# A two-layer trunk on one core: the first phase's units in another order, dt first in its last quarter

## The chip, the cores and the metric

The kernel runs on one core of one Trainium2 chip. The metric is the device time of one execution in microseconds. The kernel before takes 1793.42 us, the median of 3 runs (1793.3 to 1794.07).

## What is computed

Two layers over 256 tokens of width 2048, one after the other, and a final RMSNorm:

```python
for i in range(DEPTH):                       # 2
    mod = cond @ ada_w[i] + ada_b[i]         # cond = silu(c)
    shift, scale, gate = jnp.split(mod[:, None, :], 3, axis=-1)
    h = rmsnorm(x, norm_w[i]) * (1.0 + scale) + shift
    out = ssd_mixer(h, ...) if i == 0 else mlstm_mixer(h, ...)
    x = x + gate * out
return rmsnorm(x, final_norm_w)
```

The SSD mixer projects h to a gate z (4096), to x (4096), B and C (1024 each) and to dt (64 heads). x, B and C pass a causal convolution of 4 taps and a SiLU. dt passes a softplus; its running sum over a chunk of 128 tokens gives the decay between two tokens. A head's output is (C·B times decay) times x·dt, eight groups of eight heads. Then come the gate silu(z), a norm by group and the output projection. The mLSTM mixer projects to qk, v, o, z and to 16 gate columns, whose running sums and maxima steer the attention of each head. All weights and activations are float32.

## The kernel before

**Work and engines.** A matmul in float32 is done as three: weight and activation are split into a high and a low part, and hi·hi, hi·lo and lo·hi are summed in PSUM. `split` makes `hi` on ACT and `lo = raw - hi` on DVE, for each 128x1024 piece of weights (a weight half, 0.5 MB); `mm` then issues 24 matmuls for it (lines 298 to 300 with 256 columns of tokens, kind "fm", or 309 to 311 with 512 columns, kind "tm"). SP issues all weight loads in one queue, into six `raw` buffers; `hi` and `lo` have four each.

**Modulation.** `cond @ ada_w` is not done by matmuls. A piece of `ada_w` is loaded, and DVE adds it, times one column of cond, to an accumulator (`aacc`, line 82). After the 16 pieces of a column group `total` transposes the accumulator on TensorE (line 238) and sums each of the eight 128x128 blocks with an ACT instruction that accumulates. Its items stand between the weight items, at places that tables (`ADA_AT`, the numbers in `POST`) and the loop of layer 1 fix.

**Phase one.** Layer 0 goes through the contraction in four quarters (`START`). In each quarter nine units (`PRE`: x of groups 0 to 2, z of groups 0 to 2, and the three B·C units, of which unit j serves the two groups 2j and 2j+1) get their share of weights. The first two (`RES`) stay in PSUM banks (`pj`); the other seven leave their partial sums after every quarter, added by DVE to SBUF tiles (`park`), through banks called `ms`. dt's unit, two weight halves and one bank, is put in the last quarter ahead of the unit number `DTPOS`.

**Background.** What follows a unit (`dt_done`, `bc_done`, `xs_done`, `z_fin`, `gen_ssd`) is a generator; after each weight half all live generators take a step (`run_bg`), so their instructions fall between those of the projections. `hold` keeps note of generators that occupy a PSUM bank. The instructions' order on each engine comes from a scheduler that works on this stream. An engine runs its queue strictly in order.

**dt.** `dt_done` computes the bias, `softplus` (13 DVE operations, one exp on ACT), the scan along tokens and the rest of dtrow, sends the running sums to DRAM (`acd`, POOL queue), then transposes them (lines 564 to 566). `gen_rows` loads them back, spread over the partitions (`acb`), and `gen_decay` makes the decay tiles E on ACT.

**Groups.** `bc_done` does the convolution and then the products B·C (line 585), masked to `cbm`. From unit 1 on it waits until the SSD of group 2j-2 is over. `gen_ssd` waits for dt, B·C and x, makes X, E·cbm, the head outputs, the product with silu(z), the squares by token (`token_sq`, line 342), the group's norm (`vs`, POOL's power `rs`, `dg` on DVE, a transpose at line 335), and y.

**Layer change and after.** The last output pass of layer 0 adds gate·out to x (`xT`, DVE) and squares it; `make_h` reduces, takes the root and spreads it, and `h_chunk` makes the activations of layer 1 (`hT`). Layer 1's first phase has four quarters of eight units (`K1`). Its gates unit goes in the last quarter ahead of the first weight item; `gates_done` makes the gate rows on DVE and transposes them (lines 861, 862) three steps later. At the end `OutStat.write` scales four 128x1024 pieces and stores them from SP's queue (line 389).

Of the kernel before, what the change touches and what calls it, by code (L numbers as in the profile page):

```python
# [11 lines left out]
ALU = mybir.AluOpType  # L12

P = 128
# [14 lines left out]
NV = _o  # L29

ADA_AT = [[0, 2, 3, 3, 5, 5, 5, 7], [0, 0, 4, 5, 5, 5, 8, 8], [0, 0, 0, 1, 2, 3, 7, 8]]
DTPOS = 7
START = [4, 4, 4, 4]
K1 = [("o", 0), ("z", 0), ("qk", 0), ("v", 0), ("qk", 1), ("v", 1), ("o", 1), ("z", 1)]
RES1, DEF1, GPOS = 2, 16, 0
PRE = [('x', 0), ('z', 1), ('z', 2), ('x', 2), ('bc', 0), ('bc', 1), ('bc', 2), ('x', 1), ('z', 0)]
RES = 2
RAWB, HIB, E6B = 6, 4, 2
HP_SPLIT = (False, None)
# [11 lines left out]
def trunk_kernel(ctx, tc, xt, vecs, ada, wdt, wss, wso, wgt, wml, wmo, fnw, result):  # L51
    nc = tc.nc
# [70 lines left out]
    items = []  # L123
# [70 lines left out]
    def hold(b, banks):  # L194
        if banks[0].space == PS:
            holding.append(b)
        return b

    slots = {"s4a": 2, "s4b": 2, "s4c": 2}
# [12 lines left out]
    def ada_work(it):  # L212
        layer, key, q, w = it["layer"], it["key"], it["q"], it["w"]
        per = 1024 // w
        if q == 0:
            finish(sums)
            acc_tiles[layer, key] = sp.tile([P, 1024], F32, tag="adaacc", name=nm("aacc"), bufs=1)
        acc = acc_tiles[layer, key][:, 0:w]
        for k in range(2 * per * q, 2 * per * (q + 1)):
            raw = it["raw"][(k // per) % 2][:, (k % per) * w:(k % per + 1) * w]  # L220
            if k == 0:
                vts(acc, raw, cond[:, 0:1], None, ALU.mult)
            else:
                stt(acc, raw, cond[:, k:k + 1], acc, ALU.mult, ALU.add)
        if q != it["nq"] - 1:
            return
        if key < 4:
            spans = [(4 * key, 4), (16 + 4 * key, 4)]
        else:
            spans = [(32 + 8 * (key - 4), 4), (36 + 8 * (key - 4), 4)]  # L230
        def total():
            yield
            sm = sp.tile([P, 8], F32, tag="asum", name=nm("asum"))
            ps = [misc() for _ in spans]
            c = 0
            for t, (o, n) in zip(ps, spans):
                for b in range(n):
                    nc.tensor.transpose(t[:, b * P:(b + 1) * P], acc[:, (c + b) * P:(c + b + 1) * P], ident)
                c += n
            c = 0  # L240
            for t, (o, n) in zip(ps, spans):
                for b in range(n):
                    sl = slice(b * P, (b + 1) * P)
                    act(t[:, sl], t[:, sl], AF.Copy, accum_out=sm[:, c + b:c + b + 1])
                m = mod[layer][:, o:o + n]
                vtt(m, sm[:, c:c + n], vec(f"ab{layer}", o, n), ALU.add)
                c += n
                known.update((layer, o + b) for b in range(n))
                if 16 <= o < 32:
                    stt(amul[layer][:, o - 16:o - 16 + n], m, 1.0, vec(f"nw{layer}", o - 16, n), ALU.add, ALU.mult)  # L250
            yield
        sums.append(spawn(total()))
# [108 lines left out]
    class OutStat(RowStat):  # L361
# [18 lines left out]
        def write(self):  # L380
            r = self.column()
            for i in range(2):
                for tb in range(2):
                    o = self.o[tb][:, 1024 * i:1024 * (i + 1)]
                    if tb:
                        act(o, o, AF.Copy, scale=r[:, 1:2])
                    else:
                        vts(o, o, r[:, 0:1], None, ALU.mult)
                    nc.sync.dma_start(result[tb * P:(tb + 1) * P, 1024 * i:1024 * (i + 1)], o)

    rbt = {}

# [182 lines left out]
    def bc_done(j):  # L575
        def f(banks):
            def g():
                yield from gate_ok(lambda: j == 0 or held[0, 2 * j - 2].over)
                yield from take("s4c")
                bc = sp.tile([P, 4, T], F32, tag="s4c", name=nm("bc"))  # L580
                yield from gen_conv(banks, "scw", "scb", [32 + 2 * j, 33 + 2 * j, 40 + 2 * j, 41 + 2 * j], bc)
# [10 lines left out]
            held["bc", j] = hold(spawn(g()), banks)  # L592
        return f

    taken = set()

    def xs_done(g):
        def f(banks):
# [64 lines left out]
    def gen_ssd(g):  # L663
# [16 lines left out]
        for j in range(2):  # L680
            yield from gate_ok(lambda: (g, j) in E_t)
            E = E_t[g, j]
            vtt(E, E, cbm[g].unsqueeze(1).broadcast_to([P, 4, 384]), ALU.mult)
            yield from lag(2)
            ps = misc()
            for h in range(4):
# [102 lines left out]
    for tok in POST:  # L789
# [9 lines left out]
        for q, cnt in tok[2:]:  # L799
            mine, exq[q] = exq[q][:cnt], exq[q][cnt:]  # L800
            tail = []
            if tok[0] == "op" and q == 0:
                tail = items[n + 7:]
                del items[n + 7:]
            new = items[n:]
            out, e = [], 0
            for i, it in enumerate(new):
                out.append(it)
                while e < len(mine) and (e + 1) * len(new) <= (i + 1) * len(mine):
                    out.append(mine[e])  # L810
                    e += 1
            items[n:] = out + mine[e:] + tail
# [23 lines left out]
    def gates_done(banks):  # L836
        def g():
# [17 lines left out]
            nc.vector.tensor_tensor_scan(G, ip, ip, 0.0, ALU.max, ALU.max)  # L855
            nc.gpsimd.dma_start(Gd, G[0:8, :])
            vtt(lf, bc, G, ALU.add)
            yield from lag(3)
            p1, p2 = misc(), misc()
            for c in range(2):  # L860
                nc.tensor.transpose(p1[:, c * P:(c + 1) * P], lf[:, c * P:(c + 1) * P], ident)
# [133 lines left out]
    for q in range(4):  # L995
# [4 lines left out]
        for j, w in enumerate(new):  # L1000
            if q == 3 and j == GPOS:
                add_unit(Unit("fm", 1, 8, 1, h_act, gates_done), [wgt])
            items.append(w)
            n = -(-len(late) // max(1, len(new) - j + (2 - q) * len(new))) if q < 3 else 0
            items.extend(late[:n])
            late = late[n:]
    assert not late
# [148 lines left out]
```

## Time and profile before

| what | value |
|---|---|
| median of 3 runs | 1793.42 us |
| profiled execution | 1796.28 us, span 1794.2 us |
| mean granted TensorE clock | 0.973 |
| PE busy | 1689.0 us (94%), 13285 matmuls |
| DVE, ACT, POOL busy | 73%, 52%, 2% |
| read from HBM | 400.89 MB, 225 GB/s over the span |
| DMA queue of the loads | 64.1% of 16 engines' span |

The page shows PE near its full share and the other engines well below it. The idle time of DVE and ACT is thus no cost by itself; what counts is the idle time of PE, and who ended it. The granted clock is that of TensorE: 1 is 2.4 GHz, 0.5 is 1.2 GHz. "L82" in a row is a helper's line (`stt`), as are 78 (`act`), 86 (`vtt`) and 90 (`vts`), so rows are told apart by their tiles.

### The profile page before, as it was taken

The numbers are of one execution on the slowest core, as the hardware profiler recorded it, in microseconds if no ns is written. First come the engines' busy times: TensorE is split into PE (matmuls) and PEld (weight loads), VectorE is DVE, ScalarE is ACT, GpSimd is POOL, SyncE is SP. The second block draws the span as 40 slices with busy tenths as digits, with TensorE's granted clock in tenths as the row PEclk, the third lists the DMA queues.
The fourth block names the chain that finished last, engine by engine and source line by source line (L and its number), as shares of the span: only waits on it lengthen the run. The fifth ranks groups of instructions, "written<-read, shape, count | busy, mean of one in ns | idle before, by whom it ended". The sixth has DMA issues, their size and how long they took to land.

```text
span 1794.2 us, 32830 instructions
## 1 busy us (share of the span) xinstructions
PE 1689.0 (94%) x13285; PEld 1632.0 (91%) x13285; DVE 1301.5 (73%) x1635; ACT 928.0 (52%) x1583; POOL 36.2 (2%) x55
## 2 busy tenths in 40 slices
PE   2998999888999999979997999999999999999997
PEld 2998998888999999979897989899999999999996
DVE  6789996888986788677967886767455556564554
ACT  3443557868874674435444554544345444454433
POOL 0000000000000000000000000000000000000000
PEclk6999999989999999989998999999999999999998
DMA  9989855756876667878954666777555555555551
GB/s 358 323 298 302 298 181 181 263 188 207 288 280 212 214 221 252 277 246 302 333 199 138 206 217 228 256 237 238 198 185 173 186 170 186 185 195 175 186 180 69
DMA packets 111048, 405.20 MB, mean 226 GB/s; under 512 B 12440, under 2 KB 12448, under 8 KB 110896
## 3 DMA queue, kind: packets, MB, share of 16 engines
q1 hardware_dynamic: 107856, 392.54, 64.1%
q0 software_dynamic: 3040, 10.56, 1.9%
q8 instruction: 104, 1.70, 0.4%
q14 instruction: 48, 0.39, 0.1%
HBM read 400.89 MB, written 2.17 MB: 225 GB/s over the span
## 4 chain that ended last, share of the span: by engine, by line
PE 72%; issue 10%; DVE 9%; DMA 6%; ACT 2%; POOL 0%; SPq 0%; ACTq 0%; POOLq 0%; DVEq 0%
PE pj L298 17%; PE pj L300 17%; PE pj L299 17%; DMA raw<-in_ada 4%; DVE aacc L82 3%; DVE lo L86 3%; PE ms L298 2%; PE ms L300 2%; PE ms L299 2%; PE pj L309 2%; PE pj L310 2%; PE pj L311 2%; DMA raw<-in_wss 1%; ACT hi L78 1%; PE ms L689 1%
## 5 line engine op out<-in xcount | busy, mean ns | idle before, releaser
L78 ACT ACTIVATE hi<-raw 128x1024 fp32r<-128x1024 f32 x548 | 582.1, 1064 | 677.5 <-PE pj L299 444.0
L86 DVE TENSOR_TENSOR lo<-raw,hi 128x1024 fp32r<-128x1024 f32 x548 | 667.0, 1222 | 333.7 <-ACT hi L78 330.7
L298 PE MATMUL pj<-hT,hi 128*128 128x256 f32 x2144 | 608.2, 284 | 8.0 <-ACT hT L78 6.6
L300 PE MATMUL pj<-hT,lo 128*128 128x256 f32 x2144 | 602.7, 281 | 2.2 <-DVE lo L86 2.2
L299 PE MATMUL pj<-hT,hi 128*128 128x256 f32 x2144 | 601.6, 281 | 0.6 <-DVE hT L82 0.6
L298 PEld LDWEIGHTS pj<-hT,hi 128*128 128x128 f32 x2144 | 406.9, 190 | 11.4 <-ACT hT L78 7.4
L300 PEld LDWEIGHTS pj<-hT,lo 128*128 128x128 f32 x2144 | 406.2, 190 | 3.1 <-DVE lo L86 3.0
L299 PEld LDWEIGHTS pj<-hT,hi 128*128 128x128 f32 x2144 | 406.9, 190 | 1.1 <-DVE hT L82 0.8
L298 PE MATMUL pj<-y,hi 128*128 128x256 f32 x1024 | 292.2, 285 | 0.0
L300 PE MATMUL pj<-y,lo 128*128 128x256 f32 x1024 | 290.3, 283 | 0.0
L299 PE MATMUL pj<-y,hi 128*128 128x256 f32 x1024 | 290.1, 283 | 0.0
L82 DVE SCALAR_TENSOR_TENSOR aacc<-raw,cond,aacc 128x1024 f32<-128x1024 f32 x180 | 230.7, 1281 | 72.8 <-DMA raw<-in_ada 71.6
L298 PE MATMUL ms<-hT,hi 128*128 128x256 f32 x704 | 197.9, 281 | 3.9 <-DVE park L86 2.4
L300 PE MATMUL ms<-hT,lo 128*128 128x256 f32 x704 | 197.1, 280 | 1.7 <-DVE lo L86 1.7
L298 PEld LDWEIGHTS pj<-y,hi 128*128 128x128 f32 x1024 | 196.5, 192 | 1.0 <-issue 0.9
L299 PE MATMUL ms<-hT,hi 128*128 128x256 f32 x704 | 196.8, 280 | 0.0
L299 PEld LDWEIGHTS pj<-y,hi 128*128 128x128 f32 x1024 | 196.7, 192 | 0.0
L300 PEld LDWEIGHTS pj<-y,lo 128*128 128x128 f32 x1024 | 196.7, 192 | 0.0
L298 PEld LDWEIGHTS ms<-hT,hi 128*128 128x128 f32 x704 | 132.4, 188 | 5.9 <-DVE park L86 3.0
L300 PEld LDWEIGHTS ms<-hT,lo 128*128 128x128 f32 x704 | 132.3, 188 | 2.3 <-DVE lo L86 2.3
L299 PEld LDWEIGHTS ms<-hT,hi 128*128 128x128 f32 x704 | 132.4, 188 | 0.4
L309 PE MATMUL pj<-hi,hT 128*128 128x512 f32 x192 | 77.3, 403 | 0.0
(185 smaller groups left out, 1569.7 us busy)
## 6 DMA issues: line engine op xcount, KB each, us to landing
raw<-in_wml SPq DMA_DIRECT2D x256, 512.0 KB, 3.9
raw<-in_ada SPq DMA_DIRECT2D x192, 512.0 KB, 5.4
raw<-in_wss SPq DMA_DIRECT2D x160, 512.0 KB, 4.7
raw<-in_wso SPq DMA_DIRECT2D x64, 512.0 KB, 5.5
raw<-in_wmo SPq DMA_DIRECT2D x64, 512.0 KB, 3.8
acb<-acd POOLq DMA_DIRECT2D x16, 512.0 KB, 5.9
xT<-in_xt SPq DMA_DIRECT2D x4, 512.0 KB, 6.2
out<-o SPq DMA_DIRECT2D x4, 512.0 KB, 4.0
```

The costliest lines, as they stand in the source:

```text
L78: nc.scalar.activation(out, in_, func, **kw)
L82: nc.vector.scalar_tensor_tensor(out, a, s, b, op0, op1)
L86: nc.vector.tensor_tensor(out, a, b, op)
L298: nc.tensor.matmul(o, hi[:, w0:w0 + P], ah, start=first, stop=False, skip_group_check=True)
L299: nc.tensor.matmul(o, hi[:, w0:w0 + P], al, start=False, stop=False, skip_group_check=True)
L300: nc.tensor.matmul(o, lo[:, w0:w0 + P], ah, start=False, stop=last, skip_group_check=True)
L309: nc.tensor.matmul(o, ah[:, s], wh, start=(fresh and kk == 0), stop=False)
L310: nc.tensor.matmul(o, al[:, s], wh, start=False, stop=False)
L311: nc.tensor.matmul(o, ah[:, s], wl, start=False, stop=(kk == u.nk - 1 and (closes or (u.park is not None and ends))))
L689: nc.tensor.matmul(o, X[:, 0, xh, :], E[:, h, 0:T], start=True, stop=False, skip_group_check=True)
```

## The change

`PRE` has another order: x0 and the B·C unit 0 are now the two that stay in PSUM, and the other B·C units and x1 come earlier. `DTPOS` is 0: dt's unit is put ahead of the last quarter's first unit. `hold` moves a generator with a PSUM bank to the front of those that step. `total` sums the shift half of layer 0's groups with one DVE reduction in place of four ACT instructions. B·C unit j waits for the last use of group 2j-2's `cbm`, not for that group's end. The last output pass of layer 0 has modulation only among its first eight weight items of twelve, and layer 1's modulation starts at the fourth unit of its first quarter, not at the first. The gates' transposes come after six steps, not three. The second token half's stores are issued from ACT's queue.

```diff
--- before.py
+++ after.py
@@ -29,11 +29,11 @@
 NV = _o
 
 ADA_AT = [[0, 2, 3, 3, 5, 5, 5, 7], [0, 0, 4, 5, 5, 5, 8, 8], [0, 0, 0, 1, 2, 3, 7, 8]]
-DTPOS = 7
+DTPOS = 0
 START = [4, 4, 4, 4]
 K1 = [("o", 0), ("z", 0), ("qk", 0), ("v", 0), ("qk", 1), ("v", 1), ("o", 1), ("z", 1)]
 RES1, DEF1, GPOS = 2, 16, 0
-PRE = [('x', 0), ('z', 1), ('z', 2), ('x', 2), ('bc', 0), ('bc', 1), ('bc', 2), ('x', 1), ('z', 0)]
+PRE = [('x', 0), ('bc', 0), ('z', 0), ('x', 1), ('bc', 1), ('bc', 2), ('z', 1), ('x', 2), ('z', 2)]
 RES = 2
 RAWB, HIB, E6B = 6, 4, 2
 HP_SPLIT = (False, None)
@@ -194,6 +194,8 @@
     def hold(b, banks):
         if banks[0].space == PS:
             holding.append(b)
+            gens.remove(b)
+            gens.insert(0, b)
         return b
 
     slots = {"s4a": 2, "s4b": 2, "s4c": 2}
@@ -239,7 +241,11 @@
                 c += n
             c = 0
             for t, (o, n) in zip(ps, spans):
-                for b in range(n):
+                both = layer == 0 and key < 4 and c == 0
+                if both:
+                    nc.vector.tensor_reduce(sm[:, 0:n], t.rearrange("p (b t) -> p b t", b=4), axis=mybir.AxisListType.X,
+                                            op=ALU.add)
+                for b in range(0 if both else n):
                     sl = slice(b * P, (b + 1) * P)
                     act(t[:, sl], t[:, sl], AF.Copy, accum_out=sm[:, c + b:c + b + 1])
                 m = mod[layer][:, o:o + n]
@@ -386,7 +392,7 @@
                         act(o, o, AF.Copy, scale=r[:, 1:2])
                     else:
                         vts(o, o, r[:, 0:1], None, ALU.mult)
-                    nc.sync.dma_start(result[tb * P:(tb + 1) * P, 1024 * i:1024 * (i + 1)], o)
+                    (nc.scalar if tb else nc.sync).dma_start(result[tb * P:(tb + 1) * P, 1024 * i:1024 * (i + 1)], o)
 
     rbt = {}
 
@@ -575,7 +581,7 @@
     def bc_done(j):
         def f(banks):
             def g():
-                yield from gate_ok(lambda: j == 0 or held[0, 2 * j - 2].over)
+                yield from gate_ok(lambda: j == 0 or 2 * j - 2 in cb_used)
                 yield from take("s4c")
                 bc = sp.tile([P, 4, T], F32, tag="s4c", name=nm("bc"))
                 yield from gen_conv(banks, "scw", "scb", [32 + 2 * j, 33 + 2 * j, 40 + 2 * j, 41 + 2 * j], bc)
@@ -592,7 +598,7 @@
             held["bc", j] = hold(spawn(g()), banks)
         return f
 
-    taken = set()
+    taken, cb_used = set(), set()
 
     def xs_done(g):
         def f(banks):
@@ -681,6 +687,8 @@
             yield from gate_ok(lambda: (g, j) in E_t)
             E = E_t[g, j]
             vtt(E, E, cbm[g].unsqueeze(1).broadcast_to([P, 4, 384]), ALU.mult)
+            if j:
+                cb_used.add(g)
             yield from lag(2)
             ps = misc()
             for h in range(4):
@@ -802,6 +810,9 @@
             if tok[0] == "op" and q == 0:
                 tail = items[n + 7:]
                 del items[n + 7:]
+            if tok[0] == "op" and ip == npass:
+                tail = items[n + 8:]
+                del items[n + 8:]
             new = items[n:]
             out, e = [], 0
             for i, it in enumerate(new):
@@ -855,7 +866,7 @@
             nc.vector.tensor_tensor_scan(G, ip, ip, 0.0, ALU.max, ALU.max)
             nc.gpsimd.dma_start(Gd, G[0:8, :])
             vtt(lf, bc, G, ALU.add)
-            yield from lag(3)
+            yield from lag(6)
             p1, p2 = misc(), misc()
             for c in range(2):
                 nc.tensor.transpose(p1[:, c * P:(c + 1) * P], lf[:, c * P:(c + 1) * P], ident)
@@ -1001,7 +1012,7 @@
             if q == 3 and j == GPOS:
                 add_unit(Unit("fm", 1, 8, 1, h_act, gates_done), [wgt])
             items.append(w)
-            n = -(-len(late) // max(1, len(new) - j + (2 - q) * len(new))) if q < 3 else 0
+            n = -(-len(late) // max(1, len(new) - j + (2 - q) * len(new))) if q < 3 and (q, j) >= (0, 3) else 0
             items.extend(late[:n])
             late = late[n:]
     assert not late
```

Three places show how the queues change. The first is PE's queue around dt's transposes. In the kernel before (`ms_2944` is a parked unit's bank, `pj` a unit's that stays):

```order
L565 MATMUL ms_2929<-ident,acs 128x128 [waits DVE_49,PE_49]
L298 MATMUL ms_2944<-hT,hi_2793 128x256 [waits PE_49]
L565 MATMUL ms_2929<-ident,acs 128x128 [waits DVE_49]
L299 MATMUL ms_2944<-hT,hi_2793 128x256
L566 MATMUL ms_2929<-ident,dtrow 128x128 [waits DVE_49]
L300 MATMUL ms_2944<-hT,lo_2794 128x256
```

The transposes stand between the matmuls of a unit that has no part in dt. In the changed kernel, where `pj_2256` is dt's own bank and `ms_2493` that of unit z0:

```order
L306 MATMUL pj_2256<-hT,lo_2189 128x256
L570 MATMUL ms_2408<-ident,dtrow 128x128 [waits DVE_49]
L570 MATMUL ms_2408<-ident,dtrow 128x128
L571 MATMUL ms_2409<-ident,acs 128x128 [waits DVE_49] x2
L572 MATMUL ms_2409<-ident,dtrow 128x128 [waits DVE_49]
L304 MATMUL ms_2493<-hT,hi_2363 128x256 [waits Activation_49]
L305 MATMUL ms_2493<-hT,hi_2363 128x256
```

dt's last matmul, the transposes that wait for DVE, and the next unit's matmuls now follow each other directly.

The second place is DVE's queue ahead of the end of the convolution for B·C unit 1 (`bc_3894` before, `bc_3338` in the change; `xs_3857` is the x of group 2, `y` a finished group). Before:

```order
L82 SCALAR_TENSOR_TENSOR bc_3894<-park_649,V,bc_3894 128x255
L82 SCALAR_TENSOR_TENSOR xs_3857<-park_502,V,xs_3857 128x254
L82 SCALAR_TENSOR_TENSOR bc_3894<-park_649,V,bc_3894 128x254
L82 SCALAR_TENSOR_TENSOR xs_3857<-park_502,V,xs_3857 128x253
L82 SCALAR_TENSOR_TENSOR bc_3894<-park_649,V,bc_3894 128x253
L86 TENSOR_TENSOR lo_4046<-raw_3925,hi_4045 128x1024
L82 SCALAR_TENSOR_TENSOR xs_3857<-th_4049,xs_3857 128x512
L82 SCALAR_TENSOR_TENSOR bc_3894<-park_649,V,bc_3894 128x255
L82 SCALAR_TENSOR_TENSOR aacc_3573<-raw_3929,cond,aacc_3573 128x1024
L82 SCALAR_TENSOR_TENSOR bc_3894<-park_649,V,bc_3894 128x254
L82 SCALAR_TENSOR_TENSOR aacc_3573<-raw_3931,cond,aacc_3573 128x1024
L82 SCALAR_TENSOR_TENSOR bc_3894<-park_649,V,bc_3894 128x253
```

In the changed kernel, up to the last row of the convolution:

```order
L86 TENSOR_TENSOR lo_3552<-raw_3321,hi_3551 128x1024
L86 TENSOR_TENSOR xs_2403<-xs_2403,ms_3558 128x1024
L82 SCALAR_TENSOR_TENSOR bc_3338<-park_646,V,bc_3338 128x255
L86 TENSOR_TENSOR lo_3597<-raw_3406,hi_3596 128x1024
L86 TENSOR_TENSOR y_3602<-xs_2403,y_3602 128x4x256
L82 SCALAR_TENSOR_TENSOR bc_3338<-park_646,V,bc_3338 128x254
L82 SCALAR_TENSOR_TENSOR bc_3338<-park_646,V,bc_3338 128x253
L86 TENSOR_TENSOR lo_3639<-raw_3408,hi_3638 128x1024
L82 SCALAR_TENSOR_TENSOR bc_3338<-th_3642,bc_3338 128x512
```

The x convolution and the modulation products that alternated with its steps are gone from this stretch; parts of group 0's end stand there.

The third place is DVE's queue at the layer change, from the last residual add to the `dg` of the new layer's norm. Before:

```order
L82 SCALAR_TENSOR_TENSOR xT<-pj_8971,mod_80,xT 128x256 x2
L86 TENSOR_TENSOR lo_9261<-raw_9082,hi_9260 128x1024
L82 SCALAR_TENSOR_TENSOR aacc_9166<-raw_9164,cond,aacc_9166 128x1024
L354 TENSOR_REDUCE vs_9217<-xss_168 128x2
L82 SCALAR_TENSOR_TENSOR aacc_9166<-raw_9290,cond,aacc_9166 128x1024
L90 TENSOR_SCALAR vs_9217<-vs_9217 128x2
L82 SCALAR_TENSOR_TENSOR aacc_9166<-raw_9292,cond,aacc_9166 128x1024
L90 TENSOR_SCALAR dg_9222<-ones,rs_9220 128x128 x2
```

In the changed kernel:

```order
L82 SCALAR_TENSOR_TENSOR xT<-pj_8991,mod_80,xT 128x256 x2
L82 SCALAR_TENSOR_TENSOR xT<-pj_8992,mod_80,xT 128x256 x2
L86 TENSOR_TENSOR lo_9241<-raw_9019,hi_9240 128x1024
L90 TENSOR_SCALAR aacc_9398<-raw_9270,cond 128x1024
L360 TENSOR_REDUCE vs_9197<-xss_168 128x2
L90 TENSOR_SCALAR vs_9197<-vs_9197 128x2
L90 TENSOR_SCALAR dg_9202<-ones,rs_9200 128x128 x2
```

Of three modulation products one is left, ahead of the reduction, and it is the first of its group.
On PE, further on, the gates' transposes (lines 872 and 873 of the changed kernel) move behind one more "tm" unit of 24 matmuls.

## Rows read from the trace of the kernel before

**Rows 1.** The page: busy time by engine; granted clock in 40 slices.

```profile
PE 1689.0 (94%) x13285; PEld 1632.0 (91%) x13285; DVE 1301.5 (73%) x1635; ACT 928.0 (52%) x1583; POOL 36.2 (2%) x55
...
PEclk6999999989999999989998999999999999999998
```

**Rows 2.** Waits of PE in four stretches (255, 420, 780, 960): total, times, longest us.

```profile
PE pj L300 <- DVE lo L86: 1.6, 2, 0.9
PE pj L298 <- ACT hi L78: 0.8, 1, 0.8
...
PE ms L342 <- DVE xs L86: 6.8, 1, 6.8
...
PE ms L335 <- DVE dg L90: 5.3, 1, 5.3
PE ms L342 <- DVE xT L82: 4.5, 2, 3.9
...
PE ms L861 <- DVE gaterow L86: 10.2, 1, 10.2
```

**Rows 3.** PE's timeline after 353: start, duration, instruction, idle before and its releaser.

```profile
366.40 1.19 PE L585 MATMUL ms<-bc 128*128 128x256 f32 x2 [12.52 <-DVE bc L82]
...
371.23 0.41 PE L300 MATMUL pj<-hT,lo 128*128 128x256 f32 x1
...
371.62 0.28 PE L299 MATMUL pj<-hT,hi 128*128 128x256 f32 x1
```

**Rows 4.** Windows: length, PE, PEld, DVE, ACT, POOL busy, clock, DMA share, GB/s.

```profile
0.00:45.00 45.00, 11.01 (x54) 9.79 (x55) 30.91 (x44) 15.07 (x43) 2.91 (x9) 0.68 0.95 358
...
287.00:294.00 7.00, 5.42 (x31) 5.01 (x31) 3.12 (x3) 7.00 (x17) 0.54 (x1) 0.76 0.38 123
...
315.00:360.00 45.00, 38.88 (x337) 37.72 (x335) 39.82 (x54) 38.75 (x80) 2.36 (x4) 0.98 0.75 257
...
712.00:785.00 73.00, 72.70 (x609) 72.50 (x608) 53.27 (x58) 31.08 (x52) 0.00 (x0) 1.00 0.83 278
...
810.00:870.00 60.00, 56.77 (x429) 53.82 (x429) 47.87 (x50) 31.14 (x52) 0.00 (x0) 1.00 0.91 315
```

**Rows 5.** DVE's timeline at 968, after the unit ahead of the gates' transposes.

```profile
968.00 0.68 DVE L86 TENSOR_TENSOR park<-park,ms 128x512 f32<-128x512 f32 x1
```

**Rows 6.** DVE's timeline at the start of layer 0's activations.

```profile
40.33 1.26 DVE L82 SCALAR_TENSOR_TENSOR htmp<-xT,am,ms 128x256 f32<-128x256 f32 x3
```

**Rows 7.** DVE's timeline of dt's chain, from 257 to 274.

```profile
257.40 0.69 DVE L82 SCALAR_TENSOR_TENSOR bc<-th,bc 128x512 f32<-128x512 f32 x1
258.04 0.48 DVE L90 TENSOR_SCALAR dtrow<-pj,V 128x256 f32<-128x256 f32 x1
...
259.07 1.22 DVE L86 TENSOR_TENSOR lo<-raw,hi 128x1024 fp32r<-128x1024 f32 x1
...
260.53 1.75 DVE L413 RECIPROCAL spw<-spw 128x256 f32<-128x256 f32 x1
...
268.41 0.48 DVE L82 SCALAR_TENSOR_TENSOR xs<-park,V,xs 128x255 f32<-128x255 f32 x1
268.81 0.42 DVE L82 SCALAR_TENSOR_TENSOR spw<-spw 128x256 f32<-128x256 f32 x1
...
273.68 0.73 DVE L555 TENSOR_TENSOR_SCAN acs<-ones,dtrow 128x128 f32<-128x128 f32 x2
```

**Rows 8.** PE's timeline at dt's transposes (no idle time before them).

```profile
273.03 0.41 PE L564 MATMUL ms<-ident,dtrow 128*128 128x128 f32 x2
```

**Rows 9.** DVE's timeline at the layer change.

```profile
786.77 1.28 DVE L82 SCALAR_TENSOR_TENSOR aacc<-raw,cond,aacc 128x1024 f32<-128x1024 f32 x1 [3.54 <-DMA raw<-in_ada]
...
793.01 1.28 DVE L82 SCALAR_TENSOR_TENSOR aacc<-raw,cond,aacc 128x1024 f32<-128x1024 f32 x1
...
797.52 0.48 DVE L90 TENSOR_SCALAR dg<-ones,rs 128x128 f32<-128x128 f32 x2 [0.58 <-POOL rs L326]
```

**Rows 10.** The final stores, line 389: from issue to landing.

```profile
DMA to landing us min/median/max: 2.7/4.0/5.5
```

## The prediction

> **What bounds the kernel now.** I read the page first: TensorE (PE) is busy 1689.0 of 1794.2 us, DVE 73%, ACT 52%, and PE's clock is full in most slices [rows 1]. So time is lost only where PE idles (105 us) or runs at half clock, and the reader should ask of every edit which PE wait it touches. Apart from the head and the final norm it is in few places, which the waits by stretch name: three small waits near 271 to 289, a DVE product before the squares at 426, the layer change near 784 to 799, the gate row at 968 [rows 2], and the longest, 12.52 us before the second group pair's B·C product at 354 [rows 3]. Each long wait is paid twice. PE came back at 366.40 at 1.2 GHz, its matmuls take 0.41 us up to 371.23 and 0.28 from 371.62, when 2.4 GHz is granted again, 5.2 us later [rows 3]. Half of that, 2.6 us, is lost. For waits of 6 to 10 us I take 2 us. The windows give the clock and the traffic of the stretches, and the head: 34 of the first 45 us are idle, while the first modulation is awaited [rows 4].
>
> **Sum base.** Durations are from the profiled execution, 1796.28 us (span 1794.2 and 2.1 around it); it stands 2.9 above the median of 1793.42, and differences carry over. A measurement of this kernel tells about 0.2%, 3.6 us, from no change.
>
> **The start: -0.5.** One 128x512 reduction on DVE replaces four ACT accumulations for the shift half, four times. DVE operations of that width take 0.68 (a park add of a PSUM bank) [rows 5]. But the first `htmp` starts at 40.33 behind a product on its own queue [rows 6], so ACT's shorter queue helps little there. Bounds 0 to -2, value -0.5.
>
> **dt first: +16.8.** Before, dt's chain on DVE runs from 258.04 to 274.41: bias, softplus, a reciprocal of 1.75, scan, with other units' work between [rows 7]. The transposes that wait for it begin at 273.03 and cost PE nothing [rows 8], since over a hundred projection matmuls lie between. In the new order the five transposes stand directly behind dt's own 48 matmuls, ahead of z0's first. So PE has nothing to run while DVE makes dtrow, and the scan too. Between them DVE's queue holds dt's 19 operations, together 8.8 us by their rows, one lo (1.22), nine conv steps (0.48) and three silu products (0.69): 16.4 in all, and since each starts about 0.08 before the one ahead ends (268.41 to the next at 268.81) some 14.2 us. All of it is PE idle, plus 2.6 for the clock: +16.8. Bounds: 8.8 if the foreign rows were done already; 16.4 (the chain as it ran before) plus 2.6, or 19.0. I take the count of the new queue.
>
> **What the early dt buys: -4.1 and -23.9, with +6.0 given back.** Now E and X of the first group come in the pause. Before, they pushed hi and lo conversions out, 1.6 + 0.8 us of waits, and part of 287 to 294 ran at 1.2 GHz (granted 0.76 over 7 us, so 1.7 lost) [rows 2, 4]: -4.1, bound 0. At the second pair's B·C product, DVE interleaved two convolutions and two modulation products. In the new order no xs step stands between, and from the lo that releases PE's last 24 matmuls (712 to 785 has 609 in 72.7 us, 0.12 each [rows 4], so 2.9 us) to the last silu product DVE has four 1.22 rows, three 0.48 and one 0.69, 6.4 us in steps. The wait becomes at most 3.5 if DVE comes straight from that lo; I take 2.8, as part of it lies done by then. So -12.52 - 2.6 = -15.1, and +2.8 back. At 426 the product waited behind the third pair's conv [rows 2]; in the new order that conv lies two hundred PE rows earlier: -6.8 - 2 = -8.8. New small waits: 1 at the third pair's B·C and 2.2 at the first group's `dg` (a `dg` wait can cost 5.3, [rows 2]). So +6.0 of new waits, bounds 0 and 9.
>
> **Layer change: -2.5.** Before, the last residual adds stand behind a modulation product that waits 3.54 us for its load, and products sit between reduction, scale and `dg` (793.01 to 797.52) [rows 9]; PE idles 3.9 + 0.6 + 5.3 us. With the last pass's modulation in its first eight items and layer 1's later, only one product stands ahead of the reduction. The `xT` wait goes nearly whole, two products of 1.2 go out of the chain, but POOL and `dg` remain: -5.5 us, clock left as it is. Against it: each of those eight items now brings 2.1 MB per 5.6 us of matmuls, 374 GB/s. The windows show 358 at a share of 0.95, 278 at 0.83 and 315 at 0.91 [rows 4]. At 358 an item lasts 0.26 longer, 2.1 over eight; at 315 it is 8.5. The share of 0.91 says that 315 was not all, so I take +3, bounds 0 and 8.5. The Trainium skill (DMA: Bandwidth & Descriptors, Where 436 GB/s comes from) gives 425 GB/s for one core whose pair is idle, and about 358 as the limit of HBM per core. By the first the term is 0 and the total 1777, by the second 2; the trace, with 358, agrees with the second.
>
> **Gates: -4.9.** Before, the transposes follow a unit that ends just before 968 and wait 10.2 us [rows 2]. Now one more unit, 24 matmuls of 512 columns, twice the width of the former ones, 24 x 0.24 = 5.7 us, stands ahead of them. DVE's chain grows: one lo more, a park add of 0.68 that waits for that unit, fewer qk steps, some 11.0 instead of 10.2 [rows 5]. The wait becomes 5.3: -4.9, bounds 0 and -7. The half clock stays, as after 426's wait of 6.8.
>
> **Tail: 0.** The four stores land 2.7 to 5.5 us after their issue [rows 10]. ACT must finish both scalings before its two issues, so the last issue hardly comes earlier (-0.5 to +0.3). If a second queue had bandwidth of its own, the last landing could be the shortest, 2.7 instead of 5.5, and the term -2.8. The Trainium skill (DMA: Bandwidth & Descriptors, Issuing engines are not separate DMA queues) says against it that all queues share the same 16 engines and that a second issuer saves issue time alone; no row here shows two store queues.
>
> **Sum:** -0.5 + 16.8 - 4.1 - 15.1 - 8.8 + 6.0 - 2.5 - 4.9 + 0 = -13.1, so 1793.4 - 13.1 = 1780.
>
> **Rivals.**
> 1. *Slower: the pause is not paid back.* dt's stall stands, and DVE, which gains no time in it, is just as late at the second pair's B·C product and at the squares at 426. For it: DVE is busy 39.8 of 45 us from 315 to 360 [rows 4]. Against it: the new queue has no foreign conv before that product. It decides when DVE is more than 12 us behind PE at the second pair. Both waits back, without the 3.8 of new waits there: -13.1 + 23.9 - 3.8 = +7, 1800.
> 2. *The layer and gate edits don't do what they say.* Loads of eight dense items cost 8.5 instead of 3, and the gate wait keeps its 10.2: -13.1 + 5.5 + 4.9 = -2.7, 1790.7. For it: the share is already 0.91 to 0.95 [rows 4].
> 3. *The new small waits don't occur*, as the pause lets ACT and the loads run ahead: -13.1 - 6.0 = -19, 1774. Against it: `dg` and B·C still end on DVE. With dt's stall at its bound of 8.8 + 2.6 it is -24.5, 1769.
>
> **How the numbers follow.** Forecast 0.55, own range 1775 to 1787; rival 1 0.15; rival 2 0.15; rival 3 0.15. The range for 8 in 10 takes rivals 2 and 3 and leaves out most of rival 1 and the best ends: 1767 to 1796. Faster than 1789.8: the forecast, rival 3 and a third of rival 2, so 0.75; within 0.2%: most of rival 2 and some of rival 1, 0.11; slower 0.14.
>
> **What would show it.** In the new trace: one PE wait of 12 to 16 us ended by DVE's dtrow near 230 to 245, with half clock behind it (if under 9, rival 3; if absent, I misread the order). No wait above 4 us at the second pair's B·C product, none above 2 at the squares (if back, rival 1). At the layer change no load wait ahead of the last `xT`, a `dg` wait of 3 to 5, and in the 70 us before it PE waits of 1 to 5 us in all for hi or lo, at over 330 GB/s (if 8, rival 2). At the gates one wait of 4 to 7 us. After some 1060 us all lines should shift by one constant; a difference there would prove the sum wrong.

## The result, and the profile after

The changed kernel takes 1775.13 us, the median of 4 runs (1770.52 to 1779.86), against 1793.74 for the kernel before (4 runs, 1793.3 to 1794.87). The ratio is 0.9895, with a 95% interval of 0.9866 to 0.9925, so 18.6 us faster, 13.5 to 24 by the interval. Measured again beside the experiments it took 1779.64 (6 runs) against 1792.41 (18 runs), ratio 0.9925 (0.9909 to 0.9941), 12.8 us faster. The forecast, 1780 and 13.1 faster, lies inside the second interval and just outside the first; 1780 is also just above the slowest of the first four runs.

The profiled execution is the fastest of the four, 1770.52; that of before, 1796.28, took longer than any of its four. The differences below between these two traces add up to 25.5 us of span, and not to 18.6.

The page of the changed kernel, with the parts that answer to [rows 1]:

```profile
span 1768.7 us, 32784 instructions
...
PE 1679.2 (95%) x13285; PEld 1623.4 (92%) x13285; DVE 1301.9 (74%) x1639; ACT 923.3 (52%) x1551; POOL 35.6 (2%) x55
...
PEclk6999989999999999999999999999999999999998
```

PE's idle time falls from 105 to 89.5 us. Its busy time falls by 9.8 us with the same 13285 matmuls, since fewer of them ran at 1.2 GHz: the mean granted clock is 0.980, against 0.973.

The waits of PE in the stretches of [rows 2], at the places where the program now is (total, times, longest us):

```profile
PE ms L570 <- DVE dtrow L82: 12.9, 1, 12.9
PE ms L571 <- DVE acs L561: 0.2, 1, 0.2
...
PE pj L304 <- DVE xs L82: 2.6, 1, 2.6
PE ms L341 <- ACT hi L78: 0.7, 1, 0.7
PE ms L348 <- DVE xs L86: 0.6, 1, 0.6
...
PE ms L341 <- DVE dg L90: 3.2, 1, 3.2
PE pj L304 <- ACT hT L78: 1.1, 1, 1.1
PE ms L348 <- DVE xT L82: 0.3, 1, 0.3
...
PE ms L872 <- DVE gaterow L86: 5.3, 1, 5.3
```

A 12.9 us wait for dt's row is new. The 12.5 us wait before the B·C product of the second pair is gone, and the waits for the squares' product, the residual adds and the gate row have shrunk from 6.8, 4.5 and 10.2 to 0.6, 0.3 and 5.3.

PE's timeline at dt's transposes (start, duration, instruction, idle before and its releaser):

```profile
239.59 0.69 PE L570 MATMUL ms<-ident,dtrow 128*128 128x128 f32 x2 [12.89 <-DVE dtrow L82]
240.44 0.79 PE L571 MATMUL ms<-ident,acs 128*128 128x128 f32 x2 [0.16 <-DVE acs L561]
241.02 0.42 PE L572 MATMUL ms<-ident,dtrow 128*128 128x128 f32 x1
241.45 0.41 PE L305 MATMUL ms<-hT,hi 128*128 128x256 f32 x1
...
243.36 0.28 PE L305 MATMUL ms<-hT,hi 128*128 128x256 f32 x1
```

Projection matmuls stand behind the transposes. They were ready: in the kernel with later transposes, below, the same matmuls run without a wait until 245. Here they take 0.41 us until 2.4 GHz is granted again at 243.3, 3.7 us after PE resumed: 1.9 us more.

DVE's timeline over that wait:

```profile
226.74 0.48 DVE L90 TENSOR_SCALAR dtrow<-pj,V 128x256 f32<-128x256 f32 x1 [0.20 <-PE pj L306]
227.14 0.47 DVE L82 SCALAR_TENSOR_TENSOR bc<-pj,V,bc 128x254 f32<-128x254 f32 x1
227.53 0.42 DVE L82 SCALAR_TENSOR_TENSOR spw<-dtrow 128x256 f32<-128x256 f32 x1
227.87 1.22 DVE L86 TENSOR_TENSOR lo<-raw,hi 128x1024 fp32r<-128x1024 f32 x1
...
238.51 0.69 DVE L82 SCALAR_TENSOR_TENSOR bc<-th,bc 128x512 f32<-128x512 f32 x1
239.12 0.42 DVE L82 SCALAR_TENSOR_TENSOR dtrow<-dtrow,spw 128x256 f32<-128x256 f32 x1
...
239.96 0.74 DVE L561 TENSOR_TENSOR_SCAN acs<-ones,dtrow 128x128 f32<-128x128 f32 x2
```

dt's operations alternate with steps of two convolutions. From 226.74 to 239.54 DVE has no idle time to speak of; its queue is the wait.

The windows that answer to [rows 4] (columns as there):

```profile
315.00:360.00 45.00, 45.00 (x386) 44.90 (x385) 43.33 (x59) 34.68 (x68) 1.29 (x2) 1.00 0.65 222
...
710.00:750.00 40.00, 40.00 (x338) 39.99 (x337) 32.49 (x33) 16.39 (x30) 0.00 (x0) 1.00 0.94 343
750.00:777.00 27.00, 26.69 (x221) 26.09 (x220) 14.93 (x21) 12.58 (x22) 0.00 (x0) 1.00 0.57 196
```

PE is busy 45.00 of 45 us where it waited for B·C before. In the last pass of layer 0 the loads run at 343 GB/s, share 0.94, and PE is busy for all of 710 to 750.

**Where the time went.** Both traces hold 13285 matmul records on PE. The starts of the n-th in each, worked out from the traces (in the reordered part the n-th are not the same matmul, but the same amount of work stands before it), give the lead that the changed kernel has at that point:

| n | before, us | after, us | lead, us | what lies since the row above |
|---|---|---|---|---|
| 1500 | 229.1 | 225.8 | +3.3 | head and first three quarters |
| 1600 | 240.8 | 252.6 | -11.8 | dt's transposes |
| 2500 | 351.3 | 358.8 | -7.5 | waits at 271 to 289 of before |
| 2600 | 378.5 | 370.3 | +8.2 | B·C product of before at 354 |
| 3500 | 492.0 | 480.3 | +11.7 | squares at 426, the new bank wait at 419 |
| 5500 | 727.7 | 717.7 | +10.0 | a modulation sum at 495 |
| 6200 | 829.2 | 811.2 | +18.0 | layer change |
| 7200 | 966.5 | 950.5 | +15.9 | modulation sums of layer 1 |
| 7400 | 1008.3 | 987.7 | +20.6 | gates |
| 8600 | 1178.6 | 1154.6 | +24.0 | a q·k wait, 2.25 before and 0.85 after |
| end of span | 1794.2 | 1768.7 | +25.5 | rest and tail |

### The profile page after: what moved, and what is told of

Its sections match the earlier page's. It is cut to its first block, busy times and chain, and to the rows that moved or that the text cites. A ratio compares the mean times of both kernels' runs of the same rounds, so it can differ in the third digit from the quotient of the medians.

```text
span 1768.7 us, 32784 instructions
## 1 busy us (share of the span) xinstructions
PE 1679.2 (95%) x13285; PEld 1623.4 (92%) x13285; DVE 1301.9 (74%) x1639; ACT 923.3 (52%) x1551; POOL 35.6 (2%) x55
## 4 chain that ended last, share of the span: by engine, by line
PE 73%; issue 9%; DVE 8%; DMA 7%; ACT 2%; POOL 0%; SPq 0%; POOLq 0%; DVEq 0%; ACTq 0%
PE pj L304 18%; PE pj L305 18%; PE pj L306 18%; DMA raw<-in_ada 4%; DVE aacc L82 3%; DVE lo L86 3%; PE ms L304 2%; PE ms L305 2%; PE ms L306 2%; PE pj L315 2%; PE pj L317 2%; PE pj L316 2%; DMA raw<-in_wml 1%; ACT hi L78 1%; PE ms L697 1%
```

## The experiments

The theory is that PE's waits were moved: dt's transposes cost 15 us, the phase-one reordering gives back more than that, and layer change and gates add to it. The rivals: only the later edits gain; the pause is what lets DVE catch up; the loads limit the layer change. Three kernels undo or shift one thing in the changed kernel, five put one part into the kernel before, three build on what these showed, and one is the changed kernel again.

**The changed kernel again.** No edit.

> The changed kernel once more, to see which waits vary from run to run (its first runs spread over 9 us, those of before over 2). Theory 'phase one on the loads': the spread sits in the stretch from 45 to 230 us, where the loads run at 310 to 340 GB/s; there the time of the same matmul moves by 3 us or more between two profiles and the rest moves little. Theory 'borderline B·C wait': it sits at the second pair's B·C product or the squares after it (0 and 2.6 us in the first profile), where a wait of 3 to 9 us appears. Median 1772 to 1779 in either case.

1779.64 us (1778.65 to 1781.38, 6 runs), 0.6 above the range that I had given. Its trace is 2.3 us behind the first one at n = 1400; the same places lose more, and the bank wait of 2.59 at 419 is now:

```profile
426.53 0.55 PE L304 MATMUL pj<-hT,hi 128*128 128x256 f32 x1 [5.05 <-DVE xs L82]
```

There the lag grows to 5.1 at n = 3200. At 850 to 890 it grows by 1.6, at the q·k product near 1143 by 1.6 (a wait of 2.25 against 0.85), 8.9 at the end. So neither theory holds as it stood. The stretch up to 230 us moved by 2.3 and not by 3, and the rest by more. The wait that grew is not at the B·C product, which stayed at 0, nor at the squares, but at the PSUM bank which the x convolution of a later group still reads. What makes these waits vary was not settled. The kernel before varies too: 1787.24 to 1798.85 over 18 runs here.

**Phase one alone**, in the kernel before:

```diff
-DTPOS = 7
+DTPOS = 0
-PRE = [('x', 0), ('z', 1), ('z', 2), ...
+PRE = [('x', 0), ('bc', 0), ('z', 0), ...
+            gens.remove(b)
+            gens.insert(0, b)
-                yield from gate_ok(lambda: j == 0 or held[0, 2 * j - 2].over)
+                yield from gate_ok(lambda: j == 0 or 2 * j - 2 in cb_used)
```

> The kernel before with the phase-one part alone (order of units, dt first in the last quarter, held generators in front, the earlier release of B·C units). Theory 'moved waits': dt's pause of 13 and its clock cost 15 us, and the waits of before at 271 to 289, 354 and 426 give back 25 or so: 7 to 12 us faster than before, 1782 to 1787. Rival 'only the later edits gain': pause and gain cancel, 1791 to 1796, and the 13 to 15 us of the gain come from the layer change and the gates.

1787.2 us (10 runs), ratio 0.9969 (0.9954 to 0.9984), by the ratio 5.6 us faster. By the median it sits where both ranges nearly meet; the timeline decides for moved waits:

```profile
247.41 0.69 PE L566 MATMUL ms<-ident,dtrow 128*128 128x128 f32 x2 [12.89 <-DVE dtrow L82]
...
429.50 0.36 PE L300 MATMUL pj<-hT,hi 128*128 128x256 f32 x1 [2.62 <-DVE xs L82]
```

The two waits are those of the changed kernel to 0.03 us, the waits at 354 and 426 are gone. What this part gives is less than I expected (7 to 12). The pause is not why: in this trace it costs 15.7 us of lead (n = 1500 to 1600), and 24.4 come back until n = 3200, both as expected. Until n = 3800 4.4 are lost again, in waits for the squares, lo and the modulation (the longest 1.64, at 506), which I had not counted. The trace is that of the slowest of the ten runs, and its head alone is 4.5 behind that of before.

**dt's transposes later**, in the changed kernel:

```diff
             vts(cr, acs[:, 0:P], -1.0, acs[:, P - 1:P], ALU.mult, ALU.add)
-            yield
+            yield from lag(8)
```

> The changed kernel, but dt's transposes eight steps after its scan instead of one, so that some 125 PE rows of projections stand between dt's matmuls and them. Theory 'the transposes alone hold PE': the pause of 12.9 us and its 1.9 us of half clock go, nothing else gets worse by more than 3: 1760 to 1766. Rival 'the pause is what lets DVE catch up': the wait comes back at the first E or at the second pair's B·C product, 5 to 12 us: 1770 to 1776.

1768.9 us (4 runs), 10.7 us less than the changed kernel in the same comparison. PE's timeline:

```profile
245.55 0.38 PE L570 MATMUL ms<-ident,dtrow 128*128 128x128 f32 x2
...
246.69 0.55 PE L571 MATMUL ms<-ident,acs 128*128 128x128 f32 x2 [0.40 <-DVE acs L561]
247.09 0.33 PE L572 MATMUL ms<-ident,dtrow 128*128 128x128 f32 x1
250.43 0.55 PE L304 MATMUL ms<-hT,hi 128*128 128x256 f32 x1 [3.01 <-DVE dtT L90]
...
261.08 0.38 PE L304 MATMUL ms<-hT,hi 128*128 128x256 f32 x1 [1.25 <-DVE cbm L82]
...
269.36 0.36 PE L304 MATMUL ms<-hT,hi 128*128 128x256 f32 x1 [1.53 <-ACT hi L78]
...
417.21 0.35 PE L304 MATMUL pj<-hT,hi 128*128 128x256 f32 x1 [2.24 <-DVE xs L82]
```

The 12.89 us wait is gone. 3.01 stay: a unit waits for the bank that the transposes filled and DVE has not read. Two more follow, 1.25 for the mask of B·C and 1.53 for hi, where the changed kernel waits 0.9 at most. Against the second trace of the changed kernel this one is 15.0 us ahead at n = 1600, and 8.2 of them are gone again at n = 1800. So the pause was a loss on balance, but the rival has a part: without the pause some work behind it comes late. The waits further on do not grow. At the bank of the x convolution (2.24 here, 5.05 in that trace, 2.59 in the first) 5.6 more are gained, at a place that varies between executions. The time lies between the two expected ranges, 3 us above the first; the wait for the transposes' bank, and the two behind it, were not in it. Against the first four runs of the changed kernel it is 6.2 us less, and not 10.7.

**dt's unit back in its old place**, all else changed:

```diff
-DTPOS = 0
+DTPOS = 7
```

> The changed kernel with dt's unit put back ahead of the eighth unit of the last quarter, all else as changed. Theory 'the order of the units frees DVE at the B·C product, the early dt costs': the pause goes, no wait over 4 us at the second pair's B·C product, small hi and lo waits of 2 to 5 us near 290 come back: 1762 to 1770. Rival 'the early dt is what moves E and X out of the way of the convolutions': a wait of 8 us or more at the B·C product or the squares: 1775 to 1785.

1782.26 us (5 runs), 2.6 slower than the changed kernel beside it. No 12.9 us wait, but these:

```profile
294.51 0.58 PE L304 MATMUL pj<-hT,hi 128*128 128x256 f32 x1 [3.37 <-ACT hi L78]
...
412.83 1.22 PE L591 MATMUL ms<-bc 128*128 128x256 f32 x2 [2.10 <-DVE bc L82]
...
424.10 1.94 PE L348 MATMUL ms<-ident,xs 128*128 128x128 f32 x8 [4.41 <-DVE xs L86]
...
430.96 0.55 PE L304 MATMUL pj<-hT,hi 128*128 128x256 f32 x1 [4.93 <-DVE xs L82]
```

14.8 us of waits, each with its half clock, against 12.9 + 2.6 + 0.6 with dt early. The product at 412 is that of the third pair. The rival has the time, neither has the mechanism: the 12.5 us wait at the second pair did not come back, so with the earlier release its absence does not need the early dt; but without the early dt PE waits some 12 us more at 291 to 431, nearly what the transposes cost with it. This trace, of the slowest of the five runs, is 15.7 us ahead of the second trace of the changed kernel at n = 1800 and 3.5 behind it at n = 3200. In the medians, dt early takes 2.6 us off this kernel, and 13.4 with the transposes later as well.

**The old release of the B·C units**, all else changed:

```diff
-                yield from gate_ok(lambda: j == 0 or 2 * j - 2 in cb_used)
+                yield from gate_ok(lambda: j == 0 or (0, 2 * j - 2) in held and held[0, 2 * j - 2].over)
```

> The changed kernel, but B·C unit j waits again for the whole end of group 2j-2 (all else as changed). Its second convolution then alternates with the x convolution of group 2 again on DVE. Theory 'the earlier release is what keeps the two convolutions apart': PE waits 5 to 11 us at the second pair's B·C product near 365 and up to 3 for the clock, so 1783 to 1790. Rival 'the order of the units and the early dt do it': no wait over 4 us there, 1775 to 1780.

1784.84 us (4 runs), 5.2 more than the changed kernel's 1779.64, which was measured in another comparison; the kernel before took 1792.59 here and 1792.41 there. The time is in the first theory's range, the wait is elsewhere:

```profile
431.16 0.55 PE L304 MATMUL pj<-hT,hi 128*128 128x256 f32 x1 [9.98 <-DVE xs L82]
```

DVE's timeline ahead of that:

```profile
421.59 0.48 DVE L82 SCALAR_TENSOR_TENSOR bc<-park,V,bc 128x255 f32<-128x255 f32 x1
...
424.26 1.25 DVE L82 SCALAR_TENSOR_TENSOR xs<-pj,V,xs 128x255 f32<-128x255 f32 x3
```

PE waits 9.98 us, not at a B·C product but for the PSUM bank which an x convolution reads, the place of the 2.59 and 5.05 above. The place I named was wrong: the product was covered here too. So neither the earlier release nor, by the kernel above, the early dt is needed for that by itself. The order of the units and the held generators in front were in both kernels; whether they do it alone, no run separates. What the earlier release does is in DVE's queue. Here nine steps of the third pair's convolution stand between 409 and 432, where the second trace of the changed kernel has none; that convolution's product comes at 442.4 and not at 399.6, and the x convolution that PE waits for starts at 424.26 and not at 417.00.

**The two modulation moves alone**, in the kernel before:

```diff
+            if tok[0] == "op" and ip == npass:
+                tail = items[n + 8:]
+                del items[n + 8:]
...
-... if q < 3 else 0
+... if q < 3 and (q, j) >= (0, 3) else 0
```

> The kernel before with the two moves of modulation alone (none in the last third of layer 0's last pass, none in layer 1's first three units). Theory 'load wait out of the chain': at the layer change PE idles 4 to 5 us instead of 10.9, and half clock falls from 17 to 7 us: 7 to 8 us gained there, the denser loads before it cost under 1, and the denser modulation after it gives 1 to 4 back near 840 to 900: 1786 to 1790. Rival 'the loads are the limit': PE waits for hi or lo between 712 and 777, 3 to 8 us in all: 1790 to 1795.

1789.2 us (6 runs), ratio 0.9967 (0.9955 to 0.9978). Windows of its trace:

```profile
715.00:755.00 40.00, 40.00 (x337) 40.00 (x337) 36.33 (x36) 15.32 (x18) 0.00 (x0) 1.00 0.94 338
...
785.00:810.00 25.00, 20.42 (x153) 19.25 (x152) 19.23 (x34) 11.55 (x19) 0.69 (x1) 0.86 0.50 167
```

In the dense pass PE is busy 40.00 of 40 us at 338 GB/s, and its trace has no wait up to 777: the rival falls. Its lead over the trace of before grows by 8.4 us across the layer change (n = 5800 to 6200) and falls by 4.8 from there until n = 6800, when layer 1's denser modulation makes PE wait for sums and parked banks.

**The gates' transposes alone**, in the kernel before:

```diff
-            yield from lag(3)
+            yield from lag(6)
```

> The kernel before with the gates' transposes six steps after the rows instead of three. Theory: the wait at 968 goes from 10.2 to 5.3 us as one more unit of 5.7 us stands ahead and DVE's chain is 0.8 longer: 4.9 faster plus up to 1.5 for the clock, 1786 to 1789. Rival 'the chain waits for that unit's park add': the wait stays 9 to 10: 1792 to 1794.

1788.18 us (7 runs), ratio 0.9964 (0.9952 to 0.9975). The wait is what was expected, to the hundredth that of the changed kernel:

```profile
975.17 0.45 PE L861 MATMUL ms<-ident,gaterow 128*128 128x128 f32 x1 [5.33 <-DVE gaterow L86]
```

**The stores alone**, in the kernel before:

```diff
-                    nc.sync.dma_start(result[...], o)
+                    (nc.scalar if tb else nc.sync).dma_start(result[...], o)
```

> The kernel before with the second half's stores on ACT's queue. Theory 'one set of DMA engines': the time from the last matmul to the end goes from 12.25 us to 11.5 to 12.3, no change that a run shows. Rival 'two queues, two rates': to 9.5 or less, 2.8 faster.

1794.38 us (10 runs), ratio 1.0002 (0.999 to 1.0013). Its trace, at the end:

```profile
1780.68 1.01 SPq L389 DMA_DIRECT2D out<-o  x2
1781.08 1.38 ACTq L389 DMA_DIRECT2D out<-o  x2
```

The last issue ends 1.78 us after the first began, against 2.88 with one queue, and the tail behind PE's last matmul falls from 12.25 to 11.53. The landing takes 2.7 to 5.1 us from issue, as before [rows 10]. So the tail is 0.7 us shorter by issue time, below what the runs can tell. This is what the Trainium skill (DMA: Bandwidth & Descriptors, Issuing engines are not separate DMA queues) says, that a second issuer saves issue time alone.

**The reduction alone**, in the kernel before:

```diff
+                if both:
+                    nc.vector.tensor_reduce(sm[:, 0:n], ..., axis=mybir.AxisListType.X, op=ALU.add)
-                for b in range(n):
+                for b in range(0 if both else n):
```

> The kernel before with the shift half of layer 0's sums done by one DVE reduction. Theory: the reduction takes 0.6 to 0.7 us; the first activations start 0 to 0.5 us earlier and each of the three later groups frees its transposes' bank up to 0.5 earlier: 0 to 2 us faster, 1791 to 1794. Rival 'DVE is what the first phase waits for': the reductions come in the way of lo conversions, 1 to 3 us slower.

1792.83 us (10 runs), ratio 0.9998 (0.9988 to 1.0007), no difference. DVE's timeline:

```profile
34.99 0.69 DVE L244 TENSOR_REDUCE asum<-ms 128x4 f32<-128x512 f32 x1 [1.27 <-PE ms L238]
...
40.06 1.26 DVE L82 SCALAR_TENSOR_TENSOR htmp<-xT,am,ms 128x256 f32<-128x256 f32 x3
```

The reduction takes 0.69, and the first `htmp` still stands behind lo rows and products of its own queue: 6.2 us after the transposes may start, before 6.3.

**Both transpose groups later.** The changed kernel with dt's transposes as above and, for the gates:

```diff
-            yield from lag(6)
+            yield from lag(10)
```

> The changed kernel with dt's transposes eight steps after the scan and the gates' transposes ten steps after the rows. Theory 'each transpose group holds PE only for want of work ahead of it': the gate wait of 5.3 us and its half clock (3 us more at 1.2 GHz, 1.5 lost) go on top of what the later dt transposes gave (10.7): 1760 to 1765. Rival 'the later gate rows hold up the first attention head': 3 to 6 us come back as a wait for qk near 1000 or 1135: 1766 to 1770.

1766.77 us (5 runs), ratio 0.9843 (0.9825 to 0.9861). In its trace the gate wait is not there:

```profile
PE ms L304 <- ACT eT L78: 0.6, 1, 0.6
```

That is all that PE waits from 940 to 985, and against the kernel with dt's step alone the lead grows by 7.0 us between n = 7200 and 7400. The q·k wait near 1130 stays 2.26, so nothing came back. The median is 2.1 lower only, 1.8 above the range of the theory, and from another comparison; the intervals of the two ratios overlap. By n = 7200 this trace was 6 us behind, for one by a 2.1 us wait for lo at 832. So the gain at the gates is shown by the trace, and not by the times.

**Layer 1's modulation from its first, or its third unit**, on top of that kernel:

```diff
-... if q < 3 and (q, j) >= (0, 3) else 0
+... if q < 3 else 0
```

> As the kernel just named, but layer 1's modulation starts at its first unit again, as in the kernel before, while layer 0's last pass keeps its last third free. Theory 'the denser modulation after the layer change costs what the layer change gave': the waits for modulation sums near 840 to 900 fall by 3 to 4 us, and the products ahead of the new layer's norm cost 2 to 3 at the layer change: within 2 us of the kernel just named. Rival 'the layer change needs both moves': 4 to 6 us slower than it.

> As the first of these, but layer 1's modulation starts at its third unit instead of its fourth. Theory: no product stands between the residual adds and the new norm here either, so the layer change stays at 3 to 4 us of wait for its diagonal, and the less dense modulation takes 1 to 2 us out of the waits near 840 to 900: 1 to 2 us faster than the first. Rival: no difference above 1.

1765.5 us (4 runs) from the first unit, 1764.71 (4 runs) from the third (`(0, 2)`): no difference to 1766.77 that their spread of 3 to 7 us could show. With modulation from the first unit PE waits at the layer change again, 1.84, 3.59 and 3.13 us, but the long waits of 840 to 900 are down to one of 2.4:

```profile
774.96 0.44 PE L348 MATMUL ms<-ident,xT 128*128 128x128 f32 x2 [1.84 <-DVE xT L82]
779.37 1.11 PE L348 MATMUL ms<-ident,xT 128*128 128x128 f32 x4 [3.59 <-DVE xT L82]
783.61 0.66 PE L341 MATMUL ms<-ident,dg 128*128 128x128 f32 x2 [3.13 <-DVE dg L90]
```

Its trace loses 6.1 us against the other's until n = 6200 and has them back at n = 6800. So the later start in layer 1, a part of the change, gives nothing in the end: it moves the wait. For the third unit I expected no product between the adds and the norm, and there PE waited 1.19 and 1.15 for the adds.

## Why the prediction was right, point by point

- **dt first.** Forecast 14.2 of wait and 2.6 of clock; measured 12.9 + 0.2 and 1.9. The count of DVE's queue held row for row; the first transposes wait only for dtrow, and the 1.2 us of scan behind it overlap with them in part. The lead fell by 15.1. The kernel with later transposes shows that the cost was real, and that 6.8 of some 15 us were needless; the rest came back there as other waits.
- **What the early dt buys.** Forecast -4.1 and -15.1 at the small waits and the B·C product; the lead grew by 4.3 and 15.7. The release of the 426 product was forecast at -8.8: its wait fell from 6.85 to 0.58, but the lead grew by 3.5 only (n = 2600 to 3500), as a bank wait of 2.6 took its place. In the second trace, with 5.05 there, it grew by 0.7.
- **New waits, +6.0.** This step failed in its places: none at B·C nor at the first group's `dg` beyond 0.7. The bank that the x convolution reads was not on the list, and it is the one that cost 2.6, 5.05 and, with the old release, 9.98.
- **Layer change, -2.5.** Too small, and wrong in its parts. The +3 for the loads is 0: PE was busy 40.00 of 40 us at 343 GB/s. PE's waits fell from 10.9 to 4.6 us, near the forecast of -5.5. The clock term is not 0, since half clock lasts 6.8 us and not 17.1. The lead grew by 8.0, of which 2.1 were lost again at 840 to 900; that loss I had not in the sum. What remains is 5.9, in the second trace 4.2.
- **Gates, -4.9.** The wait of 5.3 is measured as 5.33; the lead grew by 4.7 to 5.1.
- **Start and tail.** -0.5 and 0: no difference and 0.7 us, both below what runs tell.
- **After 1060 us a constant.** Not quite: a wait for q·k near 1150 was 2.25 in one trace and 0.85 in the other. The second trace of the changed kernel has 2.25 again, so this is no effect of the change.
- **The rivals.** The first fell: the waits at 354 and 426 did not come back. The second fell in both halves. Of the third, the new waits at 415 to 437 came to 3.9 us in place of 6.0, in the second trace to 5.05. That the pause made them fewer is not shown: the kernel without it has 5.8 us of waits at 250 to 270, and no more of them after 270.

Between the two traces the lead at the end, 25.5, is 12.4 above the sum. 2.8 of that are the head, 1.5 phase one, 3.4 the layer change with its giving back (8.0 less 2.1, against 2.5), 3.4 the stretch with the q·k wait, and the rest is the tail and tenths. The second trace of the changed kernel takes back 8.9, in the head, at the bank, near 870 and at q·k, places that vary between executions. Its lead is 16.5: head 1.1, phase one 3.6 (forecast 5.2), layer change 4.2 (2.5), gates 4.7 (4.9), q·k 1.6, rest and tail 1.3. That the sum comes so near the second measurement is thus in part luck: phase one gave 1.6 less and the layer change 1.7 more, and inside the layer change a load term that was 0 and a clock term left out stand against a loss left out. What was right by its reasons is the pause, the B·C product and the gates. The three parts that gain, each put alone into the kernel before, have ratios of 0.9969, 0.9967 and 0.9964, together 0.990; the whole has 0.9895 and 0.9925, so no part of the gain is left without a place.

## What to carry to other kernels

A transpose that waits for another engine's chain stops the whole matmul queue behind it, however much ready work stands there. So put it behind as much matmul work as the chain is long: five transposes that waited cost 12.9 us here, and with them later the kernel took 10.7 us less in the same comparison. But count what the pause did for others: over half of the 15 us came back soon after as other waits, for a bank, a mask and a conversion. When a wait is taken away, ask for the next consumer of the same engine; in phase one it was in the main a PSUM bank that DVE still had to read. And moving work away from a narrow place helps only if its new place has room: layer 1's later modulation gave back what it gained.

## What the runs showed of the hardware that I had not expected

The loads reached 370 GB/s at a share of 0.95 in a stretch of 10 us (730 to 740 of the changed kernel), with PE busy for all of it:

```profile
730.00:740.00 10.00, 10.00 (x85) 10.00 (x85) 7.84 (x9) 4.24 (x4) 0.00 (x0) 1.00 0.95 370
740.00:750.00 10.00, 10.00 (x87) 9.99 (x86) 6.98 (x8) 4.58 (x16) 0.00 (x0) 1.00 0.98 358
```

I had taken 358 for the limit and a price of 3 us from it. That row is an average over 45 us. The trace of before already held the answer in its last 25 us (length, PE busy, clock, DMA share, GB/s):

```profile
20.00:45.00 25.00, 4.99 (x20) 0.50 0.98 369
```

So the 3 us came of a window that was too wide. The Trainium skill (DMA: Bandwidth & Descriptors, Where 436 GB/s comes from) gives about 358 as the limit of HBM per core; the rows of 370 and 369 are above it, so the prediction was wrong to say that the trace agrees with it. They are below 425, the other figure that the prediction names. The demand of 374, an estimate of the prediction, cost PE nothing that the trace shows, at 343 over the 40 us. The same program's time also varies more than the runs of before had led me to think, 1787 to 1799 for the kernel before over 18 runs.
